# Seven block products in place of eight in half of an MLP's down product

## The chip, the cores and the metric

One core of a Trainium2 chip runs the whole program in one launch. The metric is the device time of that core in microseconds (us). Five engines have queues of their own: TensorE (PE; its weight loads are listed as PEld), VectorE (DVE), ScalarE (ACT), GpSimd (POOL, all but unused here) and SyncE (SP), which issues the DMA transfers.

## The reference

A decoder trunk of two layers on 256 tokens of 2048 features, in fp32. Each layer adds a mixer (two kinds of attention side by side) and a squared-ReLU MLP with 8192 hidden features; the change lies in the MLP and in what it shares with the mixers.

```python
D_MODEL, SEQ, DEPTH, D_FF = 2048, 256, 2, 4 * 2048

def squared_relu_mlp(h, w1, w2):
    return jnp.square(jax.nn.relu(h @ w1)) @ w2

for layer in range(DEPTH):
    h = rmsnorm(x, ln_mix[layer])
    x = x + (even_mixer(h, ...) if layer % 2 == 0 else odd_mixer(h, ...))
    h = rmsnorm(x, ln_mlp[layer])
    x = x + squared_relu_mlp(h, mlp_w1[layer], mlp_w2[layer])
return rmsnorm(x, ln_final)
```

## The kernel before

**Halves.** Every operand of a large product is split into two halves of fewer bits, `hi` (a cast on ScalarE, L162) and `lo` (the value less `hi`, a subtraction on VectorE, L163), and a product is three passes on TensorE: hi·hi, hi·lo, lo·hi (`mm`, L166 to L172).

**Weights.** `Weights.load` (L150) brings four rows of 128 at a time by SyncE, 1 MB for 512 columns, into one of three raw buffers of 2048 columns. `Weights.get` splits two rows at a time into one of three pairs of buffers `wh`, `wl` of 1024 columns. So a raw buffer comes free after two splits, and a pair of halves when TensorE has read it.

**The MLP.** Each layer's MLP goes through four chunks of 2048 hidden features. `up(c)` makes a chunk's hidden features, feature on partition, in four blocks of 512 (`FeatGemm`, L226 and L227: the high half of the weights meets both halves of x in a matmul 512 wide, the low half meets the high half in one 256 wide). An epilogue follows each block: two copies out of PSUM on ScalarE for each two tiles of features, an add (L741), the square of the positive part (L742), a cast (L743) and a subtraction (L744). `down(c)` multiplies the chunk's hidden features by 2048 rows of the second weights, in four blocks of 512 output columns, each 96 matmuls of 512 columns (L170 to L172), and adds the result, times a factor per token, to x (L748). The order of the program is up(0), up(1), down(0), up(2), down(1) and so on; the chunk's halves have two buffers. In the last chunk of layer 0, the next layer's norm is transposed and scaled between the steps (L270, L271). In that of layer 1, the last 256 columns are done one tile of tokens after the other, so that the output leaves early.

**Order and buffers.** The program is written with pools of rotating buffers; a tile that takes a buffer waits for the readers of the tile before in it. A scheduler orders the instructions of each engine when the program is built (L839, `schedule_with_timeline_sim=True`), by dependences and a timeline of its own, and each engine then runs its queue strictly in order. PSUM has eight banks: four in pool `acc`, two each in `ptr` (transposes) and `psc` (scores); in the MLP products take turns over `acc` and `psc`.

**Names.** `raw`, `wh`, `wl`: weights as loaded and their halves; `hh`, `hl`: halves of the hidden features; `both`, `a`: the epilogue's tiles; `xx`: the halves of the normed x.

## Time and profile before

| | |
|---|---|
| time, three runs | 2240.79, 2241.18, 2241.0 us (median 2241.0) |
| profiled execution | span 2239.9 us; about 1.1 us lies outside the span |
| granted TensorE clock, mean | 0.999 |
| TensorE busy | 2224.8 us, 99% of the span |
| VectorE busy | 1318.0 us, 59% |
| ScalarE busy | 1036.4 us, 46% |
| DMA | 406.65 MB, 182 GB/s |

A span is the time from the first to the last instruction of one profiled execution. Matmuls overlap at their ends, so the mean duration of one is longer than their distance; the distance is read from a window that holds nothing else. A share of busy time is a mean over stages, so the stages are read in windows. The list of waits says what ended the idle time of an engine.

### The profile page before, as it was taken

To read this page: it belongs to the slowest core of one execution; us is meant where nothing else is said; L and a number is where in the kernel's file an instruction comes from. 1 tells how busy PE (TensorE), PEld (TensorE's weight loads), DVE (VectorE), ACT (ScalarE), POOL (GpSimd) and SP (SyncE) were. 2 spreads that over 40 slices of the span, in tenths; PEclk is the share of its full clock that TensorE was granted. 3 is DMA by queue.
4 is the path that set the end of the run, shared out by engine and by line. 5 is a ranking of instruction groups with operands and counts; after the bars stand their busy time and mean duration, and the time that the engine had idled before them with its cause. 6 is when DMAs were issued, how large, how long until landed. Compare 5 with 4: busy or idle time off the path is not lost.

```text
span 2239.9 us, 29663 instructions
## 1 busy us (share of the span) xinstructions
PE 2224.8 (99%) x12126; PEld 1913.7 (85%) x12126; DVE 1318.0 (59%) x1771; ACT 1036.4 (46%) x1369; POOL 0.2 (0%) x4
## 2 busy tenths in 40 slices
PE   8999999999999999999999999999999999999998
PEld 7899988888888888888899999888888888888887
DVE  6767665565545545655575666556565555465555
ACT  5444545555434434534444443455454344344333
POOL 0000000000000000000000000000000000000000
PEclk9999999999999999999999999999999999999999
DMA  7554545555555555555555555556555555555553
GB/s 244 177 164 148 170 137 172 183 187 187 188 188 189 188 188 190 188 188 186 188 171 170 177 164 170 173 180 204 190 181 192 189 191 188 188 187 190 188 188 132
DMA packets 207605, 406.65 MB, mean 182 GB/s; under 512 B 8614, under 2 KB 15468, under 8 KB 207340
## 3 DMA queue, kind: packets, MB, share of 16 engines
q1 hardware_dynamic: 207468, 404.75, 55.5%
q8 instruction: 95, 1.56, 0.3%
q14 instruction: 42, 0.34, 0.0%
HBM read 402.62 MB, written 2.10 MB: 181 GB/s over the span
## 4 chain that ended last, share of the span: by engine, by line
PE 99%; DMA 0%; DVE 0%; ACT 0%; SPq 0%; issue 0%; DVEq 0%
PE acc L226 21%; PE acc L172 21%; PE acc L171 21%; PE acc L170 21%; PE acc L227 11%; PE pt L236 1%; PE ps L458 1%; PE po L391 1%; PE pp L236 0%; PE po L392 0%; DMA raw<-in_e_w_in_dram 0%; PE ps L689 0%; PE ps L688 0%; DMA raw<-in_mlp_w_dram 0%; PE pi L170 0%; PE pi L171 0%
## 5 line engine op out<-in xcount | busy, mean ns | idle before, releaser
L163 DVE TENSOR_TENSOR wl<-raw,wh 128x1024 fp32r<-128x1024 f32 (+3 forms) x765 | 927.6, 1213 | 849.0 <-ACT wh L162 843.1
L162 ACT CAST wh<-raw 128x1024 fp32r<-128x1024 f32 (+3 forms) x765 | 794.5, 1039 | 1081.3 <-PE acc L172 572.1
L226 PE MATMUL acc<-xx,wh 128*128 128x512 f32 x2048 | 703.6, 395 | 0.0
L227 PE MATMUL acc<-xx,wl 128*128 128x256 f32 x2048 | 544.1, 281 | 0.0
L226 PEld LDWEIGHTS acc<-xx,wh 128*128 128x128 f32 x2048 | 378.2, 188 | 77.9
L172 PE MATMUL acc<-wh,hl 128*128 128x512 f32 (+1 forms) x1024 | 402.2, 393 | 0.0
L171 PE MATMUL acc<-wl,hh 128*128 128x512 f32 (+1 forms) x1024 | 400.0, 391 | 0.0
L227 PEld LDWEIGHTS acc<-xx,wl 128*128 128x128 f32 x2048 | 385.5, 188 | 12.5
L170 PE MATMUL acc<-wh,hh 128*128 128x512 f32 (+1 forms) x1024 | 361.0, 391 | 0.0
L171 PEld LDWEIGHTS acc<-wl,hh 128*128 128x128 f32 x1024 | 192.2, 188 | 45.8
L170 PEld LDWEIGHTS acc<-wh,hh 128*128 128x128 f32 x1024 | 191.7, 188 | 45.2
L172 PEld LDWEIGHTS acc<-wh,hl 128*128 128x128 f32 x1024 | 192.3, 188 | 44.2
L171 PE MATMUL acc<-xx,wh 128*128 128x256 f32 x768 | 216.5, 282 | 0.0
L170 PE MATMUL acc<-xx,wh 128*128 128x256 f32 x768 | 216.4, 282 | 0.0
L172 PE MATMUL acc<-xx,wl 128*128 128x256 f32 x768 | 215.5, 282 | 0.0
L171 PEld LDWEIGHTS acc<-xx,wh 128*128 128x128 f32 x768 | 144.7, 188 | 0.4
L170 PEld LDWEIGHTS acc<-xx,wh 128*128 128x128 f32 x768 | 144.7, 188 | 0.4
L172 PEld LDWEIGHTS acc<-xx,wl 128*128 128x128 f32 x768 | 144.3, 188 | 0.0
L171 PE MATMUL acc<-wl,xx 128*128 128x512 f32 (+1 forms) x320 | 127.5, 399 | 0.0
L172 PE MATMUL acc<-wh,xx 128*128 128x512 f32 (+1 forms) x320 | 125.5, 393 | 0.0
L170 PE MATMUL acc<-wh,xx 128*128 128x512 f32 (+1 forms) x320 | 119.7, 400 | 0.5 <-ACT xx L270 0.5
L171 PE MATMUL acc<-wl,oh 128*128 128x512 f32 x256 | 102.2, 399 | 0.0
(166 smaller groups left out, 1615.8 us busy)
## 6 DMA issues: line engine op xcount, KB each, us to landing
raw<-in_mlp_w_dram SPq DMA_DIRECT2D x252, 1024.0 KB, 5.1
raw<-in_o_w_in_dram SPq DMA_DIRECT2D x48, 1024.0 KB, 5.1
raw<-in_e_w_in_dram SPq DMA_DIRECT2D x35, 1024.0 KB, 5.1
raw<-in_e_w_out_dram SPq DMA_DIRECT2D x16, 1024.0 KB, 5.0
raw<-in_o_w_out_dram SPq DMA_DIRECT2D x16, 1024.0 KB, 5.1
raw<-in_mlp_w_dram SPq DMA_DIRECT2D x8, 512.0 KB, 3.8
raw<-in_e_w_uq_dram SPq DMA_DIRECT2D x4, 768.0 KB, 4.4
raw<-in_e_w_in_dram SPq DMA_DIRECT2D x4, 640.0 KB, 4.1
```

The costliest lines, as they stand in the source:

```text
L162: nc.scalar.copy(hi, raw)
L163: nc.vector.tensor_tensor(lo, raw, hi.bitcast(F32), op=ALU.subtract)
L170: nc.tensor.matmul(o, ah, bh, start=first, stop=False, **kw)
L171: nc.tensor.matmul(o, ah, bl, start=False, stop=False, **kw)
L172: nc.tensor.matmul(o, al, bh, start=False, stop=last, **kw)
L226: nc.tensor.matmul(self.o[f], wh[:, kk, fs], xx[:, k], start=k == 0, stop=False, skip_group_check=True)
L227: nc.tensor.matmul(self.o[f][:, 0, :], wl[:, kk, fs], xx[:, k, 0], start=False, stop=k == KT - 1, skip_group_check=True)
L236: nc.tensor.transpose(o, src, ident[: src.shape[0], : src.shape[0]])
L391: nc.tensor.matmul(po[0][:, h % 2, :], values(h, 0), pr[h][:, :S], start=True, stop=False)
L458: nc.tensor.matmul(o, q[:, h, t * P : t * P + P], k[:, h, : SPAN[t][1]], start=True, stop=True)
```

## The change

In `down`, two of the four blocks of 512 columns (`seven`) are computed as 2 × 2 block products in Winograd's form of Strassen's scheme: seven products of combinations of the hidden features' quarters and of the weights' quarters in place of eight of the quarters themselves. The other two stay as they were (`plain`). A pair-step of `SevenGemm` loads two rows of 512 columns, makes three VectorE adds (`L250` to `L252` after the change), splits 1792 columns and issues 21 matmuls, each 256 wide; a block has eight such steps. `result` puts the seven sums together (L269 to L274). Four steps of the plain blocks come first, then a step of `seven` and one of `plain` in turn.

For that, `up` keeps the sums of a block in eight slots per pair of tiles, four as computed and four combinations of them (`combine`, L281 to L283), and splits all eight, 2048 columns. That tile of sums is taken from the raw buffers' rotation, the epilogue copies and adds in four pieces of 256 columns, and the hidden features' halves have one buffer per block, so the order is up(0), down(0), up(1), down(1), and so on.

Weights are now split four rows at a time, 2048 columns, for all products: two buffers each of `raw`, `wh`, `wl`, and a third each from the MLP's pool inside an MLP (`in_turn`). Not shown in the diff: the constants of the mixers are loaded at the beginning of each mixer instead of once, the gains of the last norm by block, and the split of the last 256 columns eight rows at a time.

```diff
-            raw = self.flat("raw", F32, n, 3, 2048)
+            raw = raw_tile(n * self.width).rearrange("p (k n) -> p k n", n=self.width)
...
-        def get(self, k, n, into=None):
+            self.raw.append([at, n, raw, None])
+        def get(self, k, n):
             if not self.raw:
                 self.load()
...
+            at, m, raw, halves = self.raw[0]
             if k + n == at + m:
                 self.raw.popleft()
...
+            if halves is None:
+                halves = [h.rearrange("p (k n) -> p k n", n=self.width) for h in half_tiles(m * self.width)]
+                split(*halves, raw)
+                if k + n < at + m:
+                    self.raw[0][3] = halves
+            return [h[:, k - at : k - at + n, :] for h in halves]
+    more, turns = [], {"raw": count(), "wh": count(), "wl": count()}
+    def in_turn(tag, dt, n):
+        if more and next(turns[tag]) % 3 == 2:
+            return more[0].tile([P, 2048], dt, name=nm(tag), tag=tag, bufs=1)[:, :n]
+        return wpool.tile([P, 2048], dt, name=nm(tag), tag=tag, bufs=2)[:, :n]
+    def raw_tile(n):
+        return in_turn("raw", F32, n)
+    def half_tiles(n):
+        return in_turn("wh", F32R, n), in_turn("wl", F32R, n)
+    def split(hi, lo, raw):
+        nc.scalar.copy(hi, raw)
+        nc.vector.tensor_tensor(lo, raw, hi.bitcast(F32), op=ALU.subtract)
...
+    def bank(shape=(P, 512), of=acc):
+        tag = {acc: "acc", ptr: "pt", psc: "ps"}[of]
+        return of.tile(list(shape), F32, name=nm("bank"), tag=tag)
...
+    class SevenGemm:
+        PRODUCTS = ((0, 0, 1, 1), (0, 1, 6, 6), (1, 0, 4, 5), (1, 1, 5, 4), (2, 0, 2, 7), (2, 1, 7, 2), (3, 0, 3, 3))
+        def __init__(self, pool, act, pairs, src):
+            self.pool, self.act, self.steps, self.src = pool, act, pairs, src
+            self.o = None
+        def step(self, i):
+            raw = raw_tile(2048)
+            b = raw.rearrange("p (s n) -> p s n", n=256)
+            nc.sync.dma_start(raw[:, :1024].rearrange("p (k n) -> p k n", n=512),
+                              self.src[2 * i * P : (2 * i + 2) * P, :].rearrange("(k p) n -> p k n", p=P))
+            nc.vector.tensor_add(b[:, 4:6], b[:, 1:3], b[:, 0:1].to_broadcast([P, 2, 256]))
+            nc.vector.tensor_add(b[:, 6], b[:, 4], b[:, 2])
+            nc.vector.tensor_add(b[:, 7], b[:, 6], b[:, 3])
+            halves = half_tiles(2048)
+            split(*(h[:, 256:] for h in halves), raw[:, 256:])
+            bh, bl = (h.rearrange("p (s n) -> p s n", n=256) for h in halves)
+            if self.o is None:
+                self.o = [bank((P, 2, 256)) for _ in range(4)]
+            for q, j, sa, sb in self.PRODUCTS:
+                mm(self.o[q][:, j, :], self.act(i, sa), (bh[:, sb], bl[:, sb]), i == 0 and j == 0, i == self.steps - 1,
+                   skip_group_check=True)
+        def result(self):
+            (p1, p6), (p7, p5), (p4, p3), (p2, _) = ((o[:, 0, :], o[:, 1, :]) for o in self.o)
+            c1 = self.pool.tile([P, 256], F32, name=nm("c1"), tag="c1", bufs=1)
+            v = self.pool.tile([P, 2, 512], F32, name=nm("v"), tag="v", bufs=1)
+            u2, u3, u4 = v[:, 1, 256:], v[:, 0, :256], v[:, 1, :256]
+            nc.scalar.copy(c1, p1)
+            nc.vector.tensor_tensor(u2, p6, c1, op=ALU.subtract)
+            nc.vector.tensor_add(v[:, :, :256], self.o[1], u2.unsqueeze(1).to_broadcast([P, 2, 256]))
+            nc.vector.tensor_tensor(v[:, 0, 256:], p4, u3, op=ALU.subtract)
+            nc.vector.tensor_add(u3, p5, u3)
+            nc.vector.tensor_add(u4, p3, u4)
+            nc.vector.tensor_add(u2, p2, c1)
+            return [v[:, t, :] for t in range(NT)]
+    def combine(s):
+        n = s.shape[1]
+        nc.vector.tensor_tensor(s[:, :, 4:6, :], s[:, :, 0:1, :].to_broadcast([P, n, 2, 128]), s[:, :, 1:3, :], op=ALU.subtract)
+        nc.vector.tensor_tensor(s[:, :, 6, :], s[:, :, 1, :], s[:, :, 5, :], op=ALU.subtract)
+        nc.vector.tensor_tensor(s[:, :, 7, :], s[:, :, 3, :], s[:, :, 6, :], op=ALU.subtract)
...
-            self.o = [bank((P, 2, S), wide) for _ in range(4)]
+            self.o = [bank((P, 2, S), f) for f in of]
...
             def up(c):
...
+                act = []
                 for n in range(4):
                     c0 = c * 2048 + n * 512
-                    o = FeatGemm(w1[:, c0 : c0 + 512], True).run()
...
+                    if c == 0 and n == 1:
+                        flush()
+                    o = FeatGemm(w1[:, c0 : c0 + 512], [psc, psc, ptr, ptr] if n % 2 else [acc] * 4).run()
+                    sums = raw_tile(2048).rearrange("p (k s n) -> p k s n", s=8, n=128)
+                    halves = [pool.tile([P, 2, 8, 128], F32R, name=nm(h), tag=f"{h}{n}", bufs=1) for h in ("ah", "al")]
+                    for j in range(2):
+                        half = pool.tile([P, 2, S], F32, name=nm("half"), tag="half", bufs=2)
+                        a = sums[:, j, 0:4, :].rearrange("p (k t) n -> p k (t n)", t=NT)
                         for i in range(2):
...
+                            nc.scalar.copy(half[:, i], o[2 * j + i][:, 1, :])
+                            nc.vector.tensor_add(a[:, i], o[2 * j + i][:, 0, :], half[:, i])
                         nc.vector.scalar_tensor_tensor(a, a, 0.0, a, op0=ALU.max, op1=ALU.mult)
...
+                    combine(sums)
+                    split(*halves, sums)
+                    act.append(halves)
+                return act
             def add(t, cs, o):
                 nc.vector.scalar_tensor_tensor(x[:, t, cs], o, rr[:, t : t + 1], x[:, t, cs], op0=ALU.mult, op1=ALU.add)
-            def down(c, h):
+            def down(c, act):
                 last = c == NCH - 1
+                slot = lambda p, s: [h[:, p % 2, s, :] for h in act[p // 2]]
+                row = lambda k, t: slot(k // 2, 2 * (k % 2) + t)
                 blocks = [slice(n * 512, n * 512 + 512) for n in range(4)]
                 if last and tail:
                     blocks[3:] = [slice(1536, 1792)]
-                for n, cs in enumerate(blocks):
-                    o = gemm_tok(h, 16, [w2[c * 2048 : (c + 1) * 2048, cs]], wide=True)
+                src = lambda cs: w2[c * 2048 : (c + 1) * 2048, cs]
+                def plain(n):
+                    cs = blocks[n]
+                    g = TokenGemm(row, 16, [src(cs)], psc)
+                    for i in range(8):
+                        g.step(i)
+                        tick()
+                        yield
                     for t in range(NT):
-                        add(t, cs, o[t][:, : cs.stop - cs.start])
+                        add(t, cs, g.o[t][:, : cs.stop - cs.start])
                     if last:
                         done(n, cs)
+                def seven(n):
+                    cs = blocks[n]
+                    g = SevenGemm(pool, slot, 8, src(cs))
+                    for i in range(8):
+                        g.step(i)
+                        tick()
+                        yield
+                    for t, v in enumerate(g.result()):
+                        add(t, cs, v)
+                    if last:
+                        done(n, cs)
+                def chained(*gs):
+                    for g in gs:
+                        yield from g
+                one, two = chained(plain(2), plain(3)), chained(seven(0), seven(1))
+                for _ in range(4):
+                    next(one)
+                left = [two, one]
+                while left:
+                    for g in list(left):
+                        if next(g, 0) == 0:
+                            left.remove(g)
...
+            more.append(pool)
+            act = up(0)
             r = finish_norm(ss)
             rr = small.tile([P, NT], F32, name=nm("rr"))
             nc.vector.tensor_mul(rr, r, r)
+            down(0, act)
             for c in range(1, NCH):
...
+                down(c, up(c))
+            more.clear()
```

The change moves instructions on VectorE. At the passage from the first to the second block of up, last chunk of layer 0, before (L741, L742, L744 are the epilogue of the first block, L163 the subtractions of the second block's weights):

```order
L741 TENSOR_TENSOR a_896_5371<-both_895_5370 128x512
L742 SCALAR_TENSOR_TENSOR a_896_5371<-a_896_5371 128x512
L163 TENSOR_TENSOR wl_908_5425<-raw_906_5422,wh_907_5424 128x1024
L741 TENSOR_TENSOR a_898_5379<-both_897_5378 128x512
L744 TENSOR_TENSOR hl_786_4633<-a_896_5371,hh_785_4632 128x512
L742 SCALAR_TENSOR_TENSOR a_898_5379<-a_898_5379 128x512
L163 TENSOR_TENSOR wl_910_5441<-raw_906_5422,wh_909_5440 128x1024
L744 TENSOR_TENSOR hl_786_4633<-a_898_5379,hh_785_4632 128x512
```

The same place after (L826 to L283 the sums of the first block, `wl` the second block's weights, `al` the halves of the sums):

```order
L826 SCALAR_TENSOR_TENSOR raw_1103_8353<-raw_1103_8353 128x512
L281 TENSOR_TENSOR raw_1103_8353<-raw_1103_8353 128x2x256
L282 TENSOR_TENSOR raw_1103_8353<-raw_1103_8353 128x2x128
L283 TENSOR_TENSOR raw_1103_8353<-raw_1103_8353 128x2x128
L191 TENSOR_TENSOR wl_1114_8380<-raw_1112_8377,wh_1113_8379 128x2048
L191 TENSOR_TENSOR al_1105_8355<-raw_1103_8353,ah_1104_8354 128x2048
L191 TENSOR_TENSOR wl_1120_8456<-raw_1118_8453,wh_1119_8455 128x2048
L191 TENSOR_TENSOR wl_1123_8494<-raw_1121_8491,wh_1122_8493 128x2048
```

The subtractions of the second block's first weights stood between the epilogue's steps, and now stand behind it; each is twice as wide.

In down, last chunk of layer 0, before (subtractions of weights, and the two adds to x):

```order
L163 TENSOR_TENSOR wl_920_5509<-raw_916_5490,wh_919_5508 128x1024
L163 TENSOR_TENSOR wl_925_5531<-raw_923_5528,wh_924_5530 128x1024
L163 TENSOR_TENSOR wl_927_5547<-raw_923_5528,wh_926_5546 128x1024
L748 SCALAR_TENSOR_TENSOR x_74<-acc_899_5386,rr_784_4630,x_74 128x512
L748 SCALAR_TENSOR_TENSOR x_74<-acc_900_5387,rr_784_4630,x_74 128x512
L163 TENSOR_TENSOR wl_930_5565<-raw_928_5562,wh_929_5564 128x1024
```

And after, in the stretch where a product step and a plain step alternate (L250 to L252 are the adds of a product step, `128x1792` its subtraction, `128x2048` a plain set's):

```order
L191 TENSOR_TENSOR wl_1200_9120<-raw_1198_9117,wh_1199_9119 128x2048
L250 TENSOR_TENSOR raw_1201_9135<-raw_1201_9135 128x512
L250 TENSOR_TENSOR raw_1208_9192<-raw_1208_9192 128x512
L251 TENSOR_TENSOR raw_1201_9135<-raw_1201_9135 128x256
L251 TENSOR_TENSOR raw_1208_9192<-raw_1208_9192 128x256
L252 TENSOR_TENSOR raw_1201_9135<-raw_1201_9135 128x256
L252 TENSOR_TENSOR raw_1208_9192<-raw_1208_9192 128x256
L191 TENSOR_TENSOR wl_1203_9141<-raw_1201_9135,wh_1202_9140 128x1792
L191 TENSOR_TENSOR wl_1210_9198<-raw_1208_9192,wh_1209_9197 128x1792
L191 TENSOR_TENSOR wl_1218_9238<-raw_1216_9235,wh_1217_9237 128x2048
```

Adds of two product steps now stand side by side ahead of the two subtractions of 1792 columns.

## Rows read from the trace of the kernel before

**Rows 1.** The page: busy time of each engine, and the chain's shares by engine.
```profile
PE 2224.8 (99%) x12126; PEld 1913.7 (85%) x12126; DVE 1318.0 (59%) x1771; ACT 1036.4 (46%) x1369; POOL 0.2 (0%) x4
...
PE 99%; DMA 0%; DVE 0%; ACT 0%; SPq 0%; issue 0%; DVEq 0%
```

**Rows 2.** Windows: us, busy of PE, PEld, DVE, ACT, POOL, clock, DMA share, GB/s.
```profile
440.00:480.00 40.00, 40.00 (x229) 34.76 (x228) 25.03 (x27) 21.04 (x26) 0.00 (x0) 1.00 0.56 185
600.00:640.00 40.00, 40.00 (x173) 32.19 (x172) 20.58 (x19) 14.67 (x14) 0.00 (x0) 1.00 0.59 188
...
1200.00:1240.00 40.00, 40.00 (x335) 39.79 (x334) 21.97 (x23) 15.85 (x18) 0.00 (x0) 1.00 0.55 181
```

**Rows 3.** List of waits: us in total, times, longest us.
```profile
ACT wh L162 <- PE acc L226: 331.2, 194, 2.5
...
SPq L150 <- DVE wl L163: 1850.5, 350, 10.9
```

**Rows 4.** The page's groups: a weight load; busy us, mean ns, idle before.
```profile
L171 PEld LDWEIGHTS acc<-wl,hh 128*128 128x128 f32 x1024 | 192.2, 188 | 45.8
```

**Rows 5.** Groups by form, VectorE: busy us, mean ns, idle before and its releaser.
```profile
L163 DVE TENSOR_TENSOR wl<-raw,wh 128x1024 fp32r<-128x1024 f32 x739 | 905.1, 1225 | 826.9 <-ACT wh L162 821.3 <-PE pp L236 4.8
...
L741 DVE TENSOR_TENSOR a<-both 128x512 f32<-128x512 f32 x64 | 43.8, 685 | 0.0
...
L748 DVE SCALAR_TENSOR_TENSOR x<-acc,rr,x 128x512 f32<-128x512 f32 x62 | 43.6, 743 | 0.8 <-PE acc L172 0.8
L271 DVE SCALAR_TENSOR_TENSOR xx<-pt,gains,xx 128x256 fp32r<-128x256 f32 x64 | 29.9, 480 | 13.9 <-ACT xx L270 13.1
...
L312 DVE TENSOR_TENSOR tk<-ra,rb 128x256 f32<-128x256 f32 x4 | 1.7, 422 | 0.1
```

**Rows 6.** Groups by form, ScalarE.
```profile
L162 ACT CAST wh<-raw 128x1024 fp32r<-128x1024 f32 x739 | 774.8, 1049 | 1049.7 <-PE acc L172 544.8 <-PE acc L226 331.2 <-PE acc L171 147.4
...
L162 ACT CAST wh<-raw 128x512 fp32r<-128x512 f32 x10 | 6.2, 619 | 12.5 <-PE acc L172 8.1 <-DMA raw<-in_e_w_in_dram 4.4
L595 ACT ACTIVATE rl<-pi 128x256 f32<-128x256 f32 x16 | 5.3, 378 | 0.7 <-PE pi L172 0.6
```

**Rows 7.** Timeline of ScalarE and VectorE in up: start us, us, instruction, idle before.
```profile
559.45 1.05 ACT L162 CAST wh<-raw 128x1024 fp32r<-128x1024 f32 x1
...
560.54 1.23 DVE L163 TENSOR_TENSOR wl<-raw,wh 128x1024 fp32r<-128x1024 f32 x1 [0.28 <-ACT wh L162]
561.68 0.68 DVE L741 TENSOR_TENSOR a<-both 128x512 f32<-128x512 f32 x1
```

**Rows 8.** DMA issues of the MLP's weights: KB each, median us to landing.
```profile
raw<-in_mlp_w_dram SPq DMA_DIRECT2D x252, 1024.0 KB, 5.1
...
raw<-in_mlp_w_dram SPq DMA_DIRECT2D x8, 512.0 KB, 3.8
```

**Rows 9.** Chain of waits, in time: first matmuls of two blocks of up.
```profile
432.64 0.94 PE acc L226 x4
...
455.21 0.93 PE acc L226 x4
```

**Rows 10.** Timeline of TensorE at the start of the kernel.
```profile
11.34 0.63 PE L171 MATMUL acc<-wl,xx 128*128 128x512 f32 x1
11.77 0.63 PE L170 MATMUL acc<-wh,xx 128*128 128x512 f32 x1
...
15.86 0.39 PE L172 MATMUL acc<-wh,xx 128*128 128x512 f32 x1
16.09 0.40 PE L171 MATMUL acc<-wl,xx 128*128 128x512 f32 x1
```

**Rows 11.** Windows at the end, columns as in rows 2.
```profile
2230.00:2235.00 5.00, 0.64 (x6) 0.43 (x4) 4.55 (x20) 1.76 (x4) 0.00 (x0) 0.88 0.56 210
2235.00:2239.90 4.90, 0.00 (x0) 0.00 (x0) 0.40 (x2) 0.25 (x1) 0.00 (x0) 0.50 0.57 214
```

More of the change, by code (lines that the diff above doesn't have):

```diff
@@ L81, in nm, with load_constants @@
         return f"{s}_{uid[0]}"
-    cst = cpool.tile([P, sum(n for _, n in CONSTS)], F32, name="cst")
-    C, at = {}, 0
-    for name, n in CONSTS:
-        C[name] = cst[:, at : at + n]
-        at += n
-    ident = C["ident"]
+    ident = cpool.tile([P, P], F32, name="ident")
+    C, mix = {}, []
+    def load_constants(pool, names):
+        at, n = {}, 0
+        for name, w in CONSTS:
+            at[name] = n
+            n += w
+        t = pool.tile([P, sum(dict(CONSTS)[name] for name in names)], F32, name=nm("cst"))
+        n = begin = 0
+        for i, name in enumerate(names):
+            w = dict(CONSTS)[name]
+            C[name] = t[:, n : n + w]
+            n += w
+            if i + 1 == len(names) or at[names[i + 1]] != at[name] + w:
+                nc.sync.dma_start(t[:, begin:n], const[:, at[name] + w - (n - begin) : at[name] + w])
+                begin = n
     x = cpool.tile([P, NT, D], F32, name="x")
@@ L172, in mm, with by_rows, __init__ @@
         nc.tensor.matmul(o, al, bh, start=False, stop=last, **kw)
-    turns = count()
-    def bank(shape=(P, 512), wide=False):
-        if wide and next(turns) % 6 >= 4:
-            return psc.tile(list(shape), F32, name=nm("acc"), tag="ps")
-        return acc.tile(list(shape), F32, name=nm("acc"), tag="acc")
+    def bank(shape=(P, 512), of=acc):
+        tag = {acc: "acc", ptr: "pt", psc: "ps"}[of]
+        return of.tile(list(shape), F32, name=nm("bank"), tag=tag)
+    def by_rows(act):
+        ah, al = act
+        return lambda k, t: (ah[:, k, t * P : t * P + P], al[:, k, t * P : t * P + P])
     class TokenGemm:
-        def __init__(self, act, nk, srcs, wide=False, loads=None):
-            self.act, self.nk = act, nk
+        def __init__(self, act, nk, srcs, of=acc, loads=None):
+            self.act, self.nk = act if callable(act) else by_rows(act), nk
             self.w = Weights(srcs, nk, loads)
             self.width = self.w.width
-            self.o = [bank(wide=wide) for _ in range(NT)]
+            self.o = [bank(of=of) for _ in range(NT)]
             self.steps = nk // 2
@@ L211, in decoder_trunk, with __init__ @@
     class FeatGemm:
[L215 removed]
+        def __init__(self, src, of):
             self.w = Weights([src], KT)
[L217 removed]
+            self.o = [bank((P, 2, S), f) for f in of]
             self.steps = KT // 2
@@ L324, in fill_tables @@
         for t in range(NT):
-            diag = wpool.tile([P, P], F32, name=nm("diag"), tag=("ra", "rb")[t], bufs=1)
+            diag = mix[-1].tile([P, P], F32, name=nm("diag"), tag=("ra", "rb")[t], bufs=1)
             nc.vector.tensor_scalar_mul(diag, ident, r[:, t : t + 1])
@@ L488, in load_gains @@
     def load_gains(at, gs):
-        rows = wpool.tile([P, P], F32, name=nm("rows"), tag="ra", bufs=1)
+        rows = mix[-1].tile([P, P], F32, name=nm("rows"), tag="ra", bufs=1)
         n = 0
```

79 lines of the change are left out of this document (28 added, 51 removed).

## The prediction, made before the changed kernel ran

> **What bounds the kernel now.** I read the page's busy shares first and its chain of waits second. [rows 1]: TensorE works in 99% of the span and the chain that ended last is TensorE for 99% of it, so the time before is the sum of the matmuls and nothing else. The profiled span is 2239.9 us; about 1.1 us lies outside it, as the median of the runs, 2241.0, shows. The windows by stage say what the sum is made of [rows 2]: in a down product 173 matmuls of 512 columns fill 40 us, 0.232 us each; in a stretch of heads, where all are 256 wide, 335 fill 40 us, 0.119 us each. In both VectorE works half the time. The list of waits [rows 3] shows the preparation of weights (a cast on ScalarE, then a subtraction on VectorE) waiting for TensorE to free its buffers, 194 times behind the up product alone, and TensorE, busy for all but 15 us, waits nowhere for it: operands are ready early everywhere. So two questions decide: how much TensorE work goes, and whether the operands of what is left are still early.
>
> **TensorE's own work.** A block of 512 columns took 96 × 0.232 = 22.3 us. Seven products of 3 passes on 8 pair-steps are 168 matmuls of 256 columns, 168 × 0.119 = 20.0 us. 16 of the 32 blocks change (in the last chunk the 256-wide rest stays plain), so 2.3 × 16 = 37 us go if everything else is hidden: 2241 − 37, about 2204. The Trainium skill ("Perfetto Trace Analysis", section "Identifying the Most-Contended Engine") speaks against even this: it calls matmul busy time a poor measure and wants the weight loads' busy share. A load takes 188 ns [rows 4]; by loads laid end to end a seven-block would be 168 × 0.188 = 31.6 us, and a down 23 us longer than by matmuls. The heads' window [rows 2] disagrees: 334 loads, each recorded 188 ns, fit in 40 us beside 335 matmuls, so they overlap, and I use 0.119.
>
> **Durations for the added work.** Casts and subtractions grow along a line: a subtraction of 512 columns takes 0.685 us and of 1024 1.225 [rows 5], so 1792 take 2.03 and 2048 2.30 (estimates along that line); an add of 256 takes 0.422. Casts take 0.619 and 1.049 [rows 6], so 1.70 for 1792 and 1.91 for 2048; a copy of 256 about 0.38. A subtraction starts 0.04 us behind its cast's end, and independent VectorE instructions overlap by 0.09 [rows 7]. A load of 1 MB lands 5.1 us after its issue, of 512 KB 3.8 [rows 8].
>
> **Up: from one block to the next.** One block takes 455.21 − 432.64 = 22.57 us [rows 9], four weight sets of 5.64, with no gap between blocks: in the old order the next block's subtractions stand among the epilogue's short steps. In the new order I see three kinds of passage, about eight of each in the 24 (8 ups × 3). Let T be the end of a block's last matmul. Copy 0.38, add 0.42, square 0.69, the combinations 0.69 + 0.42 + 0.42, three such hops: the sums are done at T + 3.1.
> First kind (the rows of order from layer 0's last chunk): the first set's subtraction stands behind all of this and ends at T + 5.4. TensorE can do its four matmuls with the high half, 4 × 0.232 = 0.93 us, and then waits 4.5 us.
> Second kind: the third set's weights land in the buffer that held the sums. Cast 1.91 and subtraction 2.30 of the sums end at T + 7.35, the load at T + 12.5, its cast at 14.4, its subtraction at 16.7; TensorE wants it after two sets and four matmuls, at 11.28 + 0.93 = 12.2. It waits 4.5 us.
> Third kind: the second set's subtraction stands behind the sums (T + 5.4), and the third set's load behind it: 10.5, 12.4, 14.7. It waits 2.5 us.
> 8 × (4.5 + 4.5 + 2.5) = 92 us. TensorE never wins this back, since it was the bound. Ends: nothing, if these places in the order don't bind as I read them; 7 us each (4.5 and 2.5 in one passage), 168.
>
> **Down.** Before: 384 × 0.232 = 89.2 us. After, TensorE needs about 84.8. Of VectorE's work each of 16 product steps takes 0.685 + 2 × 0.422 + 2.03 = 3.56 us, together 56.9; 6 plain sets after the first two 13.8; two results 2.8 each less what falls behind the last set, 2.8; six additions to x of 0.743, 4.5: 78 us, less 4 for overlap. It can't start before the first product step has landed, in a buffer that the second plain set frees at T + 5.4: with 3.8 for the load T + 9.2. The order puts each 1792-wide subtraction close behind its own adds, so VectorE also waits for the cast (1.70, less what stands between, often the adds of a second step): together about 6.5 us a down, and 1 us for a late load. The last set is ready at 9.2 + 74 + 6.5 + 1 = 90.7. The next up's first bank is freed by the first instruction of the second result, behind two subtractions of 2.30 and 0.42 itself: 95.7. That is 6.5 us over 89.2; eight times 52, and 12 steps of the next norm (0.48 each by the row of 256 columns, 5.8 us) ride in layer 0's last down: 58 us. VectorE, which had half its time free, is the bound of these stretches. Ends: 4.5 us less than before in each if TensorE sets the pace (−36), and 13.6 more if every second product step waits its whole cast (+109, with the norm 115).
>
> **Mixers.** Their weights are now split 2048 wide in two buffers instead of 1024 wide in three. From the moment that TensorE frees a buffer, cast and subtraction take 1.91 + 2.30, and 5.64 − 4.21 = 1.4 us are left for other work on either engine; before, two of three halves were ahead, 5.64 − 2.30 = 3.3. Where the order has longer other work between subtractions (rotations, softmax, selection), the part beyond that is TensorE's wait. By the order with the by-form durations it is 27 us beyond 3.3 and 116 beyond 1.4, for both mixers. Heads' work mostly comes in pieces that earlier slack takes up, so I take 27; ends 0 and 116.
> Loading constants again and the final gains by block is some ten small loads on a queue that waits for VectorE most of the time (1850 us, [rows 3]); nothing, and at the worst one load of 3.8 us. The last 256 columns change little.
>
> **Sum.** 2239.9 + 92 + 58 + 27 = 2417 of span, and 1.1: 2418 us. The 37 us of matmuls are inside the down term. All low ends give 2205, all upper ends 2640.
>
> **Rivals.**
> 1. *Up is covered, down is not.* The first and third sets come early enough, as before; only VectorE's downs and the mixers remain: 2241 + 58 + 27 = 2326. For it: VectorE has 40% of its time free in up [rows 2]. Against: the passages turn on the place in the order and on one buffer, not on the load.
> 2. *The other side: TensorE still sets the pace.* If the preparation runs one set ahead at each passage (the buffers freed some 5 us earlier than I read) and the 78 us of VectorE's work starts with the down, it ends before TensorE's 84.8. Then 2204, and up to 2233 if the mixers take 27. It decides from the point where VectorE's work in a down, waits included, stays under 84.8 us. For it: its bare work does.
> 3. *The clock.* Before, TensorE worked without a gap and its clock stayed full; after its last matmul the granted clock was 0.88 in the next 5 us and 0.50 after [rows 11]. At the start the matmuls of 512 columns come 0.43 us apart at 11.3 us and 0.23 at 15.9 [rows 10]: half the pace, the lower of the two clock levels, for the first 7 us or so of matmuls, which loses about 3.6 us (an estimate). If the 16 gaps of 4.5 us each drop the clock and cost as much: 2418 + 58 = 2476; with every wait in downs and mixers too, some 56, 2618. Against: no gap of this length stands in the trace before. The Trainium skill ("TensorE: Matmul & The Clock Gate", section "HAM oscillation — how this bites in real kernels") describes just such gaps between tiles that leave each next tile cold; no row here shows it between two products.
> 4. *Only the first kind of passage costs*, 8 × 4.5 = 36 us, and TensorE's gain of 37 stands beside it: 2240, no change.
> 5. *Weight loads bind* (the rule above): TensorE's down is 84.8 + 23 = 108, 12.3 over VectorE's 95.7; 98 us more, 2516.
>
> **Chances.** Forecast 0.50, with its own range 2350 to 2470; the first rival 0.15, the second 0.10, the clock 0.18, the fourth 0.04, the fifth 0.03. The range of 8 in 10 takes in the first rival, the clock at 16 gaps and the fifth: 2290 to 2530; outside it lie the second, the fourth, and the clock beyond 16 gaps. 0.2%, 4.5 us, is about what a measurement of this kernel tells from no change. Faster 0.10, the second rival; same 0.03, most of the fourth; slower 0.87.
>
> **What would show it.** TensorE's share under 95%, and in its waits two large groups: the first and third sets' matmuls in up behind the 2048-wide subtraction, 2.5 to 5 us each, some 24 times; and in down many short ones behind the 1792-wide subtraction, with VectorE busy over 80% there. One up block, 22.57 us, should become 25 to 27; a down about 95. I am wrong if up blocks stay at 22.6, if a down takes under 89 us, or if the granted clock leaves 1.0 in mid-kernel.

## The result

The changed kernel takes 2627.62 us (median of four runs, 2625.08 to 2633.73) against 2241.09: slower by a ratio of 1.173 (95% interval 1.1713 to 1.1747). The prediction had the direction right, but 2627.6 lies above its range of 2290 to 2530.

The profiled execution has a span of 2625.3 us, 385.4 more. Its page: busy shares, the clock by slices, and the chain's shares by engine.

```profile
PE 2336.8 (89%) x13278; PEld 2034.0 (77%) x13278; DVE 1666.4 (63%) x2056; ACT 1058.2 (40%) x1030; POOL 0.2 (0%) x4
...
PEclk9999999899889989999999999988998989898888
...
PE 42%; DVE 25%; DMA 21%; ACT 8%; issue 3%; SPq 0%; ACTq 0%; DVEq 0%
```

TensorE's share fell from 99% to 89%, the chain is TensorE for 42% only [rows 1], and the clock row (PEclk, in tenths of full speed) shows eights in both MLPs. Now by stage, where a stage runs from the first matmul of its kind to that of the next. Windows of the eight ups of the changed kernel: one of them, and the sum of all (columns as in rows 2).

```profile
629.70:748.60 118.90, 101.95 (x512) 86.01 (x512) 59.67 (x59) 39.53 (x34) 0.00 (x0) 0.89 0.38 129
...
sum 912.90, PE 794.69 PEld 671.68 DVE 474.71 ACT 323.17 POOL 0.00; mean PE 99.34 PEld 83.96 DVE 59.34 ACT 40.40 POOL 0.00
```

And the eight downs, the last with the end of the kernel.

```profile
748.60:857.50 108.90, 91.98 (x528) 81.21 (x528) 84.43 (x91) 45.91 (x28) 0.00 (x0) 0.94 0.49 164
...
sum 894.60, PE 746.87 PEld 654.44 DVE 695.46 ACT 377.68 POOL 0.00; mean PE 93.36 PEld 81.80 DVE 86.93 ACT 47.21 POOL 0.00
```

Before, the ups lay in 718.4 us with TensorE busy for all of it, and the downs with the end in 729.8, busy for 720.4. TensorE idles 912.9 − 794.7 = 118 us in the ups and 894.6 − 746.9 = 148 in the downs (9 before). But its busy time rose too: 76 us in ups for the same matmuls, and 63 in downs over 720.4 − 37. Most of that second part is the clock. In the trace the lower of TensorE's two levels is granted for 306 us in all, in some 50 stretches. TensorE is busy in 235 us of them, at half pace, and so loses 118 us. Where the other 31 us come from was not settled:

| us over before | ups | downs and end | mixers | sum |
|---|---|---|---|---|
| TensorE idle | 118 | 138 | 17 | 273 |
| TensorE busy for longer at the matmuls left | 76 | 63 | 9 | 149 |
| of it by the lower clock | 64 | 45 | 9 | 118 |
| matmuls removed | | −37 | | −37 |
| all | 195 | 165 | 26 | 385 |

One passage, from the first to the second block of layer 0's second up. TensorE (start, us, instruction, idle before and its releaser):

```profile
654.55 0.28 PE L308 MATMUL bank<-xx,wl 128*128 128x256 f32 x1
657.09 1.21 PE L307 MATMUL bank<-xx,wh 128*128 128x512 f32 x4 [2.26 <-ACT wh L190]
662.54 0.58 PE L308 MATMUL bank<-xx,wl 128*128 128x256 f32 x1 [4.25 <-DVE wl L191]
662.92 0.63 PE L307 MATMUL bank<-xx,wh 128*128 128x512 f32 x1
...
666.01 0.39 PE L307 MATMUL bank<-xx,wh 128*128 128x512 f32 x1
```

It waits 2.26 us for the first set's cast and 4.25 for its subtraction. Then a matmul of 512 columns takes 0.63 us (662.92), and 0.39 again from 666.01. The clock in these windows:

```profile
655.00:660.00 5.00, 1.21 (x4) 0.67 (x4) 4.90 (x10) 2.04 (x2) 0.00 (x0) 0.91 0.00 0
660.00:665.00 5.00, 2.46 (x8) 2.23 (x9) 4.69 (x3) 1.90 (x1) 0.00 (x0) 0.50 0.28 72
665.00:670.00 5.00, 5.00 (x28) 4.37 (x27) 0.40 (x1) 1.91 (x1) 0.00 (x0) 0.91 0.93 348
```

So TensorE works at half pace from 662.5 to 665.9 and loses some 1.7 us beside the wait. What the preparation did (SyncE's issue, ScalarE's casts and the last copy of the first block, VectorE's subtractions of weights and, at 662.40, of the sums):

```profile
646.68 0.92 SPq L158 DMA_DIRECT2D raw<-in_mlp_w_dram  x2
...
651.88 1.90 ACT L190 CAST wh<-raw 128x2048 fp32r<-128x2048 f32 x1 [7.56 <-DMA raw<-in_mlp_w_dram]
...
654.87 0.37 ACT L824 COPY half<-bank 128x256 f32<-128x256 f32 x1 [0.26 <-PE bank L308]
655.14 1.90 ACT L190 CAST wh<-raw 128x2048 fp32r<-128x2048 f32 x1
...
630.36 2.28 DVE L191 TENSOR_TENSOR wl<-raw,wh 128x2048 fp32r<-128x2048 f32 x1
...
644.36 2.29 DVE L191 TENSOR_TENSOR wl<-raw,wh 128x2048 fp32r<-128x2048 f32 x1 [9.06 <-ACT wh L190]
...
660.20 2.28 DVE L191 TENSOR_TENSOR wl<-raw,wh 128x2048 fp32r<-128x2048 f32 x1
662.40 2.29 DVE L191 TENSOR_TENSOR al<-raw,ah 128x2048 fp32r<-128x2048 f32 x1
```

The subtraction that ends at 646.65 frees a raw buffer, and two loads go out at 646.68. The order on SyncE's queue shows which:

```
L158 DMA raw_735_5215<-in_mlp_w1_dram 128x4x512
L158 DMA raw_750_5315<-in_mlp_w1_dram 128x4x512
L158 DMA raw_747_5277<-in_mlp_w1_dram 128x4x512
```

747 is the first set of the second block, 750 the second. 747's buffer has been free since 632.6 (the subtraction at 630.36), but its load stands behind that of 750, which waits for the one that ends at 646.65. In the same stretch SyncE's list of waits has:

```profile
SPq L158 <- DVE wl L191: 15.6, 1, 15.6
```

So 747 is cast at 655.14, behind 750, and subtracted at 660.20, behind the sums. Its cast stands behind the block's last copy too (654.87), which waits for the block's last matmul: that copy and the cast, 0.37 and 1.90 us, are the 2.26 us.

### The profile page after: what moved, and what is told of

It reads as the page before. It is cut to its first block, busy times and chain, and to the rows that moved or that the text cites. A ratio compares the mean times of both kernels' runs of the same rounds, so it can differ in the third digit from the quotient of the medians.

```text
span 2625.3 us, 31699 instructions
## 1 busy us (share of the span) xinstructions
PE 2336.8 (89%) x13278; PEld 2034.0 (77%) x13278; DVE 1666.4 (63%) x2056; ACT 1058.2 (40%) x1030; POOL 0.2 (0%) x4
## 4 chain that ended last, share of the span: by engine, by line
PE 42%; DVE 25%; DMA 21%; ACT 8%; issue 3%; SPq 0%; ACTq 0%; DVEq 0%
DMA raw<-in_mlp_w_dram 21%; DVE wl L191 15%; PE bank L198 11%; PE bank L199 11%; PE bank L197 10%; ACT wh L190 7%; PE bank L307 5%; PE bank L308 3%; DVE al L191 2%; DVE raw L250 1%; DVE raw L826 1%; DVE raw L825 1%; ACT ah L190 1%; DVE x L833 1%; DVE raw L251 1%
## 5 line engine op out<-in xcount | busy, mean ns | idle before, releaser
L191 DVE TENSOR_TENSOR wl<-raw,wh 128x2048 fp32r<-128x2048 f32 (+3 forms) x450 | 977.6, 2186 | 720.5 <-ACT wh L190 705.3
L190 ACT CAST wh<-raw 128x2048 fp32r<-128x2048 f32 (+3 forms) x450 | 812.3, 1822 | 1244.1 <-DMA raw<-in_mlp_w_dram 416.3
L307 PE MATMUL bank<-xx,wh 128*128 128x512 f32 x2048 | 759.7, 418 | 92.2 <-ACT wh L190 72.5
L308 PE MATMUL bank<-xx,wl 128*128 128x256 f32 x2048 | 583.6, 297 | 45.2 <-DVE wl L191 45.2
L307 PEld LDWEIGHTS bank<-xx,wh 128*128 128x128 f32 x2048 | 406.3, 200 | 187.4 <-ACT wh L190 81.3
L198 PE MATMUL bank<-wl,ah 128*128 128x512 f32 (+1 forms) x1440 | 472.2, 337 | 73.4 <-DVE wl L191 72.8
L308 PEld LDWEIGHTS bank<-xx,wl 128*128 128x128 f32 x2048 | 416.4, 203 | 73.0 <-DVE wl L191 62.6
L199 PE MATMUL bank<-wh,al 128*128 128x512 f32 (+1 forms) x1440 | 464.2, 331 | 0.0
L197 PE MATMUL bank<-wh,ah 128*128 128x512 f32 (+1 forms) x1440 | 415.5, 333 | 46.9 <-ACT wh L190 40.7
L197 PE MATMUL bank<-xx,wh 128*128 128x256 f32 x768 | 217.5, 285 | 7.3 <-DVE v L269 5.9
L198 PE MATMUL bank<-xx,wh 128*128 128x256 f32 x768 | 217.4, 285 | 1.9 <-DVE xx L352 1.9
L199 PE MATMUL bank<-xx,wl 128*128 128x256 f32 x768 | 214.8, 286 | 0.0
L197 PEld LDWEIGHTS bank<-xx,wh 128*128 128x128 f32 x768 | 146.7, 191 | 8.1 <-DVE v L269 6.1
L198 PEld LDWEIGHTS bank<-xx,wh 128*128 128x128 f32 x768 | 147.3, 192 | 2.4 <-DVE xx L352 2.1
L199 PEld LDWEIGHTS bank<-xx,wl 128*128 128x128 f32 x768 | 145.0, 191 | 0.2
L250 DVE TENSOR_TENSOR raw<-raw 128x512 f32<-128x512 f32 x128 | 88.3, 690 | 74.2 <-DMA raw<-in_mlp_w_dram 73.9
```

The lines of the kernel that those rows point to most:

```text
L190: nc.scalar.copy(hi, raw)
L191: nc.vector.tensor_tensor(lo, raw, hi.bitcast(F32), op=ALU.subtract)
L197: nc.tensor.matmul(o, ah, bh, start=first, stop=False, **kw)
L198: nc.tensor.matmul(o, ah, bl, start=False, stop=False, **kw)
L199: nc.tensor.matmul(o, al, bh, start=False, stop=last, **kw)
L250: nc.vector.tensor_add(b[:, 4:6], b[:, 1:3], b[:, 0:1].to_broadcast([P, 2, 256]))
```

## The experiments

Unless said otherwise, times are medians of two runs beside 2240 to 2241 of the kernel before; windows show one up and one down in the middle of layer 0, and ranges over downs leave out the last one, which holds the end of the kernel.

**The sums' place and the products.** First, no products:

```diff
-                    g = SevenGemm(pool, slot, 8, src(cs))
+                    g = TokenGemm(row, 16, [src(cs)], acc)
```

> The changed kernel with all four column blocks of down plain; buffers, epilogue, sums and combinations as changed. Theory 1 (buffers and the order of loads and subtractions starve TensorE, product or no product): up stays near 113 us each, down goes from about 109 to about 100, total about 2540. Theory 2 (the product steps' work on VectorE is what is late, and ups inherit it): ups back to 90, downs to 90, total about 2320.

Measured 2456.1.

```profile
617.90:725.80 107.90, 96.95 (x511) 82.45 (x510) 55.84 (x50) 39.69 (x33) 0.00 (x0) 0.92 0.39 129
725.80:821.70 95.90, 92.61 (x389) 74.20 (x388) 49.04 (x32) 34.48 (x19) 0.00 (x0) 0.96 0.61 206
```

Ups stay long without any product; downs of 96 instead of 109. Then the sums out of the raw rotation, with two raw buffers and then with three:

```diff
-                    sums = raw_tile(2048)...
+                    sums = pool.tile([P, 2048], F32, name=nm("sums"), tag="sums", bufs=1)...
...
-        if more and next(turns[tag]) % 3 == 2:
+        if more and tag != "raw" and next(turns[tag]) % 3 == 2:
```

> The changed kernel with the epilogue's sums in a buffer of their own and two raw buffers left for the weights; the same memory. If the sums' place in the raw rotation makes the third set of a block late: up falls by about 4 us a passage, total about 2530. If the number of raw buffers is what counts: slower than 2627, about 2700, downs longer too.

Measured 2552.7.

```profile
627.20:718.70 91.50, 90.88 (x512) 78.56 (x512) 63.07 (x58) 43.20 (x36) 0.00 (x0) 1.00 0.58 190
718.70:843.20 124.50, 98.44 (x528) 84.03 (x529) 82.28 (x91) 42.81 (x27) 0.00 (x0) 0.92 0.40 131
```

The whole loss of the ups is gone (idle 0.6 us, clock 1.00), and downs are longer with two raw buffers. Both expectations came true, one in each stage. With three (only the first of the two edits, and one buffer for the last norm's gains):

> The changed kernel with the epilogue's sums in a buffer of their own and all three raw buffers for weights (8 KB more; the last norm's gains in one buffer instead of two). Ups as in the run with two raw buffers, 91.5 us each. Downs: if the number of raw buffers sets their pace, between the 109 of the change and less, about 105, total about 2400; if VectorE's amount of work sets it, also 109 and not less, since that was the same with two buffers in neither; if two or three raw buffers make no difference and something else made 125, about 125 and 2550.

Measured 2372.4, 255 us less than the change.

```profile
601.90:692.70 90.80, 90.80 (x513) 79.54 (x514) 62.17 (x59) 40.40 (x34) 0.00 (x0) 0.98 0.55 181
692.70:793.10 100.40, 88.66 (x531) 78.61 (x529) 81.84 (x90) 44.49 (x28) 0.00 (x0) 0.97 0.50 164
```

With three buffers and no products:

> Sums in their own buffer, three raw buffers, and all four blocks of down plain. Ups 91 each, as with the products. If the products' preparation is what the downs of 101 us lack: downs at 92 or less, total about 2290. If the start of down behind the last epilogue, which up and down one after the other bring, costs as much: downs 96 as in the run with plain blocks and the sums in a raw buffer, total about 2325.

Measured 2264.3.

```profile
590.00:679.00 89.00, 89.00 (x513) 78.09 (x512) 58.33 (x51) 41.28 (x34) 0.00 (x0) 1.00 0.59 189
679.00:768.20 89.20, 89.20 (x386) 72.13 (x385) 46.96 (x31) 32.65 (x18) 0.00 (x0) 1.00 0.57 189
```

So up and down one after the other cost nothing: of the two cases expected, downs of 92 or less and downs of 96, it is the first. The four together: with products 2627.6 and 2372.4 (sums in the rotation, sums apart), without 2456.1 and 2264.3. The sums' place costs 255 or 192 us, the products 172 or 108, all else 23.

**The order of loads and of the program.**

```diff
-                nc.sync.dma_start(raw[...], ...)
+                tc.keep_in_program_order(nc.sync.dma_start(raw[...], ...))
```

> The changed kernel with every load of weights kept in the order of its use on SyncE's queue; nothing else written differently. Theory 1a (a load that is wanted first stands in the queue behind one that waits for a buffer): passages in up lose 3 to 5 us less each, ups near 100, fewer falls of the clock, total about 2480 to 2540. Theory 1b (the place of the subtraction behind the epilogue and the sums' buffer are enough): within 25 us of 2627.

Measured 2589.9: 38 us less, between the two cases. In the ups TensorE idles for 99 us instead of 118, so the load out of order is part of the ups' loss, and the smaller part. With `schedule_with_timeline_sim=False`:

> The changed kernel with each engine's instructions in the order in which they are written, without the scheduler's reordering. If the scheduler's order is what starves TensorE: faster than 2627. If the written order puts all preparation behind epilogues, which the scheduler only softens: up passages wait for a load, cast and subtraction, 10 us or more each, and mixers lose most, over 2900.

Measured 2620.3 (2612.7 to 2628.0), ups 116 to 125, downs 97 to 110: neither expectation. The written order loses as much, so the scheduler's order is not by itself the cause.

**The clock.** In the kernel before, a pause ahead of 24 blocks of up, with `range(1)` and with `range(3)`:

```diff
...
+                        for _ in range(3):
+                            z1 = pool.tile([P, 512], F32, name=nm("z"), tag="z", bufs=2)
+                            nc.gpsimd.tensor_copy(z1, z)
+                            z = z1
...
+                        hold.append(tc.keep_in_program_order(nc.tensor.transpose(pz[:, 0, :P], z[:, :P], ident)))
+                        with tc.issue_after(hold[-1].ins):
```

> The kernel before with a pause of TensorE forced ahead of each of the 24 passages of up: one GpSimd copy of 512 columns of the epilogue's tile, which a small transpose ahead of the block waits for. No other work is lacking. Each pause is some 2 us. Theory (the clock falls in long pauses only) and rival (a pause costs its length) agree here: 24 x 2 = 48 us, 2290, granted clock 1.00.

> The same with three such copies in a chain, a pause of some 4.5 us at each passage. If a pause costs its length alone: 24 x 4.5 = 108 us, 2350. If pauses of this length drop TensorE's clock, as after the products of the changed kernel: 2 to 4 us more each, 2400 to 2440, and the mean granted clock below 0.98.

Measured 2272.8 and 2383.0. An up with short pauses, then one with long pauses and the passage in it:

```profile
677.60:770.60 93.00, 90.93 (x516) 78.56 (x515) 53.05 (x53) 44.48 (x53) 1.84 (x3) 1.00 0.55 181
```

```profile
706.00:814.30 108.30, 96.83 (x516) 83.27 (x515) 54.62 (x53) 44.74 (x53) 10.68 (x9) 0.94 0.47 156
755.00:760.00 5.00, 1.95 (x12) 1.45 (x10) 4.57 (x5) 3.74 (x7) 2.83 (x3) 1.00 0.52 153
760.00:765.00 5.00, 4.23 (x16) 3.66 (x17) 2.55 (x4) 0.62 (x1) 0.71 (x1) 0.66 0.18 68
765.00:770.00 5.00, 5.00 (x30) 4.35 (x29) 1.97 (x2) 2.10 (x2) 0.00 (x0) 1.00 0.24 63
...
760.77 0.47 PE L743 MATMUL pt<-cst,z 128*128 128x128 f32 x1 [3.82 <-POOL z L740]
...
761.68 0.63 PE L226 MATMUL acc<-xx,wh 128*128 128x512 f32 x1
...
762.32 0.63 PE L226 MATMUL acc<-xx,wh 128*128 128x512 f32 x1
...
764.17 0.40 PE L226 MATMUL acc<-xx,wh 128*128 128x512 f32 x1
...
764.52 0.40 PE L226 MATMUL acc<-xx,wh 128*128 128x512 f32 x1
```

Short pauses (0.65 to 1.25 us; shorter than expected) add 31 us of span, of which 22 are idle: 0.4 us more each, at a mean granted clock of 0.999. Long ones (3.2 to 3.9 us, most 3.8) add 144, of which 91 are idle: 2.2 us more each, with the 512-wide matmuls after 760.77 0.64 us apart where they are 0.35 from 764.17. The lower level is granted behind 23 of the 24, and TensorE is busy in 96 us of it, so 48 us, 2.0 a pause, are the clock. No load, cast or subtraction is late here, so pauses of this length by themselves bring the lower level, and in the changed kernel the clock cost 118 us beside 273 of more idle time. The Trainium skill ("TensorE: Matmul & The Clock Gate", section "HAM oscillation — how this bites in real kernels") says of gaps between tiles that the next tile then starts at the lower clock. These runs agree, by the 0.64 us behind the pause.

**The mixers.** The kernel before with `Weights.get` splitting four rows in two buffers of 2048, raw two buffers:

```diff
-            raw = self.flat("raw", F32, n, 3, 2048)
+            raw = self.flat("raw", F32, n, 2, 2048)
...
+                halves = [self.flat(h, F32R, m, 2, 2048) for h in ("wh", "wl")]
```

> The kernel before with its weights split four rows at a time in two buffers of 2048 (raw two buffers too), nothing else changed. If the mixers' 26 us come from this and the MLP has work enough ahead: 2267, all of it in the mixers. If two wide buffers starve the MLP as well: 4 us at each of 24 passages in up, falls of the clock, 2370 or more.

Measured 2253.2 (three runs). Its mixers, then those of the changed kernel (before: 400.6 and 391.1 us):

```profile
0.00:409.60 409.60, 396.85 (x2307) 348.62 (x2308) 258.65 (x472) 190.29 (x281) 0.20 (x4) 0.99 0.51 167
1129.60:1520.90 391.30, 391.30 (x2517) 353.89 (x2516) 232.81 (x307) 164.76 (x192) 0.00 (x0) 1.00 0.52 172
```

```profile
0.00:409.70 409.70, 397.09 (x2306) 348.41 (x2307) 258.52 (x472) 190.17 (x281) 0.20 (x4) 0.99 0.50 167
1306.10:1714.20 408.10, 398.16 (x2524) 359.45 (x2524) 237.69 (x320) 167.13 (x200) 0.00 (x0) 0.98 0.51 171
```

The first mixer's 9 us are the wide splits, the second mixer's 17 are not.

**The downs with products.** What makes 100 us of TensorE's 85? Four raw buffers and two pairs of halves, then the same with the product's adds on GpSimd:

```diff
+        if more and tag == "raw" and next(turns[tag]) % 4 >= 2:
+            return more[0].tile([P, 2048], dt, name=nm(tag), tag=tag, bufs=2)[:, :n]
...
-            nc.vector.tensor_add(b[:, 4:6], ...)
+            nc.gpsimd.tensor_add(b[:, 4:6], ...)
```

> As the one with own sums, but four raw buffers and two instead of three pairs of halves inside the MLP. If raw buffers set the pace of down: about 95 each, total about 2320. If three pairs of halves were needed: downs longer than 109, total over 2430. If VectorE's work and its waits for casts set it: 96 to 109.

> As the one before with four raw buffers, and the product steps' three adds on GpSimd instead of VectorE, which loses 16 x 1.53 = 24 us of work a down. If VectorE's work sets the pace of down: 10 to 20 us less per down than with the adds on VectorE. If buffers and latency set it: no better, and worse by what GpSimd is slower.

Measured 2488.3 and 2461.2. A down of each, and GpSimd's groups of the second:

```profile
707.60:825.90 118.30, 95.51 (x531) 81.16 (x529) 83.48 (x91) 46.59 (x29) 0.00 (x0) 0.93 0.43 146
```

```profile
705.20:816.00 110.80, 92.67 (x530) 79.49 (x528) 71.80 (x45) 46.56 (x29) 64.85 (x45) 0.97 0.46 156
```

```profile
L250 POOL TENSOR_TENSOR raw<-raw 128x512 f32<-128x512 f32 x128 | 232.4, 1816 | 1834.1 <-DMA raw<-in_mlp_w_dram 1739.3 <-issue 82.2 <-DVE wl L191 9.3
```

The third pair of halves was needed: 118 us instead of 100. Taking 12 us of busy time from VectorE gains 2 to 8 us a down, though an add of 512 columns takes 1.8 us on GpSimd instead of 0.69. Then loads in order and other banks for the first block of up, on three raw buffers:

```diff
-                    o = FeatGemm(w1[:, c0 : c0 + 512], [psc, psc, ptr, ptr] if n % 2 else [acc] * 4).run()
+                    o = FeatGemm(w1[:, c0 : c0 + 512], [psc, psc, ptr, ptr] if n % 2 == (c == 0) else [acc] * 4).run()
```

> Sums in their own buffer, three raw buffers, loads kept in the order of use, and the first block of an up that follows a down accumulates in the banks of the plain blocks and of the transposes instead of those that the products leave last. The wait of 2 to 4 us at the end of each down for the first step of the result goes: 7 x 3 = 21 us less than the 2372 without these two, 2350. If the order of loads binds in down as well: 2330. If the plain blocks' banks come free no earlier: 2372.

Measured 2369.7: downs of 97 to 103 but for the last of each layer, and in sum no gain that can be told. But the first mixer is 6 us longer and the second, counted from the last down, 17, where TensorE is busy for 2.3 us in the first 13; the MLPs together are 23 us shorter, by the banks or by the ordered loads, which this run does not part. VectorE's order pinned by hand, so that a step's load, adds and cast (`prep`) stand ahead of the subtraction and the matmuls of the step before (`step`), with two products and with one (four runs each):

```diff
...
+                            todo[k + 1][0].prep(todo[k + 1][1])
                         g.step(i)
...
```

> Own sums, three raw buffers, loads in order inside the MLP, the banks as in the run before, and in down VectorE's adds and subtractions pinned one step ahead: the adds of a product step stand ahead of the subtraction of the step before it, so that its cast runs under that; two plain steps ahead instead of four, so that plain steps last to the end. If the bunched order (adds of two or three steps side by side, then their casts) is what VectorE and TensorE wait for: downs 86 to 90, total about 2265. If VectorE's amount of work (78 us and its waits) sets the pace whatever the order: downs stay at 96 to 101, total about 2370.

> The same with one product block and three plain ones: VectorE's work in a down falls from 78 to about 64 us, TensorE's own from 84.8 to 87.0. If VectorE's amount of work sets the pace with two: downs 87 to 88, total about 2255, faster than the version with two. If order and latency do: downs above 90 here too.

Measured 2516.1 and 2347.7: downs of 105 to 127, and 97. The order by hand is worse, and with it the second run says nothing on the amount of VectorE's work. Four raw buffers with three pairs of halves (small tiles share a buffer to make room), then also the other banks:

```diff
+        if more and (next(turns[tag]) % 4 >= 2 if tag == "raw" else next(turns[tag]) % 3 == 2):
+            return more[0].tile([P, 2048], dt, name=nm(tag), tag=tag, bufs=2 if tag == "raw" else 1)[:, :n]
```

> The kernel with own sums and three raw buffers (2372), with a fourth raw buffer inside the MLP and still three pairs of halves; the room comes from small tiles that share a buffer (the epilogue's copies in one buffer instead of two, the result's tile in that of the sums). If a down lacks raw buffers, each of which is held about 9 us per set (load 3.6 to 5.1, adds 1.5, cast 1.7 to 1.9, subtraction 2.0 to 2.3), 24 sets and three buffers: downs 88 to 93, total about 2290. If VectorE's amount of work or its order sets the pace: downs 99 to 102, total 2365 to 2375.

> The same, and the first block of an up that follows a down in the banks of the plain blocks and the transposes. If the wait for the products' banks at the end of a down is all that it moves: 2 to 4 us less per down, 15 to 25 us less than the run without it.

Measured 2323.3, between the two cases, and 2276.7, twice the gain expected (four runs each; the second's ratio to before 1.0157, 1.0142 to 1.0172). A down of the first, an up and a down of the second:

```profile
690.60:786.80 96.20, 87.25 (x530) 77.96 (x528) 81.17 (x90) 46.66 (x30) 0.00 (x0) 0.98 0.55 185
```

```profile
592.80:681.80 89.00, 89.00 (x514) 78.28 (x513) 64.50 (x61) 42.88 (x35) 0.00 (x0) 1.00 0.58 195
681.80:771.70 89.90, 86.55 (x531) 77.91 (x529) 78.34 (x88) 44.19 (x28) 0.00 (x0) 0.98 0.54 179
```

49 us for one raw buffer, 47 for the banks, with VectorE's work as it was. Last, trims of that version, and the pinned order with four raw buffers:

> The version with own sums, four raw buffers and the other banks (2277), and three trims: the last chunk of each layer without products, the first two products of the kernel's first mixer loaded two rows at a time, and loads in order of use inside the MLP. Last down back by 12 us, the start by 6, ups by 1 each: about 2250. Below 2241 only if the downs with products come under 87 as well.

> The same with VectorE's order in down pinned one step ahead, as in the run that was slower with three raw buffers (126 us a down). If that run was slow since the pinned order holds a raw buffer longer and three were too few: downs of 86 to 88 now, total 2235 to 2245. If the pinned order is bad by itself: downs over 95, total over 2290.

Measured 2284.6 and 2355.2 (four runs each). The first mixer became 11 us longer, not shorter, and ate the 4 us gained elsewhere; 6 of the 11 stand in every run with ordered loads (415 us), also without two-row loads. With the pinned order an up and the down behind it together take 184 to 197 us (195 to 217 with three raw buffers, 177 to 184 with four and no pin): it lacked a buffer, and is slower by itself too; why was not settled. No version beats the kernel before.

## Why the prediction was wrong

The forecast of the span, 2417 us, was 208 too short. 59 of it are idle time of TensorE (26 more than forecast in ups, 43 in downs, 10 less in mixers). The other 149 are TensorE busy for longer at the same matmuls, 118 of them by the lower clock. So the step that failed most is that the sum put the clock at nothing, for no other reason than that no gap of this length stood in the trace before; the second is the bound of down.

**TensorE's 37 us.** In the 2277 version a down has 86.55 us of busy TensorE at a clock of 0.98: the removed matmuls are about what was worked out.

**Up, 92 us.** The mechanism stood. In the trace each of the 24 passages waits, eight of each kind: 47, 33 and 29 us in sum where the forecast had 36, 36 and 20. The first kind's 4.5 us was 4.25 in the passage shown (2.05 to 4.45 in the eight), VectorE's subtraction behind the sums. What was left out there is ScalarE, with the first set's cast behind the block's last copy: 2.26 us or more in each of the eight, 18 in all. Ordered loads don't change this wait; they bring the one for the subtraction down to 1.2 to 2.1 us. In sum 118 us of idle time, 26 over. That the sums' buffer is the root, which the second kind of passage said, is shown: with the sums apart and three raw buffers the weights' subtractions stand between the steps of the sums again, and no up idles over 1.1 us but one (4.8).

**Down, 58 us net.** This step failed too. I summed VectorE's work to 78 us plus 7.5 of waits behind a late start, and made it the bound. In the down shown VectorE is busy 84.4 of 108.9 us, where before it had half its time free [rows 2], and it waits for loads and casts all along (start, us, instruction, idle before):

```profile
756.48 0.69 DVE L250 TENSOR_TENSOR raw<-raw 128x512 f32<-128x512 f32 x1 [0.84 <-DMA raw<-in_mlp_w_dram]
757.20 0.43 DVE L251 TENSOR_TENSOR raw<-raw 128x256 f32<-128x256 f32 x1
757.66 0.43 DVE L252 TENSOR_TENSOR raw<-raw 128x256 f32<-128x256 f32 x1
759.89 2.03 DVE L191 TENSOR_TENSOR wl<-raw,wh 128x1792 fp32r<-128x1792 f32 x1 [1.81 <-ACT wh L190]
762.56 2.29 DVE L191 TENSOR_TENSOR wl<-raw,wh 128x2048 fp32r<-128x2048 f32 x1 [0.64 <-ACT wh L190]
765.52 0.69 DVE L250 TENSOR_TENSOR raw<-raw 128x512 f32<-128x512 f32 x1 [0.67 <-DMA raw<-in_mlp_w_dram]
```

The resource that I didn't price is the raw buffer. A set holds one for its load, adds, cast and subtraction, 3.6 + 1.5 + 1.7 + 2.0 us for a product step and 5.2 + 1.9 + 2.3 for a plain set; 24 such sets in three buffers fill 24 × 9 / 3 = 72 us of a down even if each starts the moment its buffer is free. That is a floor, under TensorE's 85, and does not give the size. Downs measured 124 us with two raw buffers, 100 with three, 96 with four, and about 90 when the banks no longer bind. VectorE's amount of work was not the bound: in that down of 89.9 us it is still busy for 78.34, and TensorE for 86.55. Idle time was 138 us where the forecast had 58 + 37 = 95.

**Mixers, 27 us.** 26 measured, and by chance: two wide buffers cost 9 in the first mixer and nothing in the second. What the second mixer's 17 us are was not settled; it took 395 to 402 in most versions with three raw buffers, so part of it isn't the split.

**The clock.** It stood as a rival at 0.18 and not in the sum: 118 us of the 385, and the granted clock leaving 1.0 in mid-kernel was named as a sign of being wrong. Its price of 3.6 us a pause was too high (2.0 to 2.2 measured), its count of 16 too low (some 50 stretches at the lower level). The price came from the start of the kernel [rows 10], where matmuls run at half pace but the trace's clock rows show no lower level. The forecast with the measured idle time alone would be 2241 + 273 − 37 = 2477, inside the range; with all of the 149 us, 2626. The upper case of that rival, 56 pauses and 2618, was the nearest of all, and the range stopped short of it. Its count was about right; that its sum is so near is luck, a price too high standing in for the idle time that was lacking.

**The other rivals.** Up covered: false, ups lost 195. Only the first kind of passage: false, all three wait. TensorE sets the pace: false as changed; with sums apart, four raw buffers and other banks downs are 88 to 94, still no gain over 89.6. Weight loads: a down of 89.9 us with the same loads excludes a least time of 108.

## What to carry to other kernels

A buffer that is borrowed from the rotation that feeds the bound engine is paid in every round: count, for each buffer, how long a tile holds it (load, each step, the wait for the next engine) and how many tiles pass in a stage, beside the busy time of the engines. Price pauses of TensorE of several us with the clock that they lose as well: here 118 us beside 273 of idle time, while pauses of about 1 us lost none. And where an engine's queue is ordered at build time, read the DMA queue's order too, for a load that stands behind one whose buffer is not yet free.

## What the runs showed of the hardware

Behind 23 of 24 pauses of TensorE of 3.2 to 3.9 us the lower clock level was granted, and 2.0 us a pause were lost by it; 24 pauses of 0.65 to 1.25 us left the mean granted clock at 0.999. GpSimd adds of 512 columns took 1816 ns against 690 on VectorE, and VectorE's subtractions of 1792 columns went from 2021 to 2293 ns in that run.
